# Weight splits for the next large products, queued ahead of a small expert's activation

## The chip, the cores and the metric

One core of a Trainium2 chip runs the whole program as one launch. The metric is the device time of that launch in microseconds, as the median of several runs. Five engines matter here: TensorE (PE, with its weight loads as PEld), VectorE (DVE), ScalarE (ACT), GpSimd (POOL) and SyncE (SP), whose queue issues nearly all weight loads.

## The reference, cut to what matters

A two-layer encoder trunk on 512 tokens of width 1024. Each layer ends with a mixture of 16 experts; a router gives every token two of them. Only the experts are touched here:

```python
y = zeros((512, 1024))
for e in range(16):
    he = silu(t @ w_gate[e]) * (t @ w_up[e])          # 1024 -> 512
    y = y + combine[:, e:e + 1] * (he @ w_down[e])    # 512 -> 1024
```

All data are fp32. The weights of one expert are 6 MB, so a layer's experts read about 100 MB.

## The kernel before, in words

**Experts in an order of their own.** The tokens of an expert are gathered by index (an indirect DMA issued by GpSimd), multiplied, and added to the output by an indirect scatter. The experts run at positions 0 to 15. Their order is drawn up so that experts with few tokens ("few": at most 64 rows, or at most 32) stand between those with more ("full": a 128-row tile). The program holds one branch for each of several mixes of sizes. With these inputs layer 0 takes the branch 15: few experts at positions 0, 6, 12 and 13 (64 rows) and 3, 5, 8, 10, 14 and 15 (32 rows). Layer 1 takes the branch 12: few experts (64 rows) at positions 0, 1, 2, 5, 8, 11, 14 and 15.

**Two products for each expert.** `A` is the first one (gate and up), `B` the second one (down). `A(e + 1)` is put into the program before `B(e)`, so that the activation of one expert lies beside a product of another. Inside `A(e + 1)` a call `mid` turns (transposes) the activated rows of expert `e`; inside `B(e)` it turns the gathered rows of `e + 2`.

**Full experts** (`stageA`, `stageB`) multiply in a fast fp32 format, in which one product is made of three: each weight slab of 128x1024 is split into a rounded part `wh` (a copy on ScalarE, L110) and a rest `wl` (a subtraction on VectorE, L111). `A` needs eight splits (four steps of gate and up), `B` four. Step `k` of a product can't start before its split. The parts live in two small pools (`wsp`, three tiles each of `wh` and `wl`; `wsp2`, two each), from which `spool()` deals in turn, so that five splits can be alive at a time. The matmuls are at L1018 to L1023 (`A`) and L1049 (`B`).

**Few experts** (`Few.a`, `Few.b`) use the raw weights, side by side in column groups of TensorE (L1092), and need no split. After the first product ScalarE applies silu (L1106) and VectorE multiplies by the up part and the token's weight (L1107); TensorE then turns the result `he` (L1079).

**Who sets the order on an engine.** The framework's planner puts all instructions of a branch into one queue for each engine, by their place in the program and by its own estimate of when each is ready. An engine then runs its queue in that order. `self.after(x, y)` is an edge that only says: `x` goes behind `y` in the queue. It adds no semaphore.

**Loads.** Each expert's 12 slabs of 512 KB are issued by SP (L122) in a fixed order, each into the slot of an earlier slab, so a load waits until that slab's last reader is done: for a full expert the split, for a few expert the matmul.

Of the kernel before, what the change touches and what calls it, by code (L numbers as in the profile page):

```python
# [8 lines left out]
F32 = mybir.dt.float32  # L9
# [3 lines left out]
AF = mybir.ActivationFunctionType  # L13
ALU = mybir.AluOpType
# [7 lines left out]
NE = 16  # L22
# [22 lines left out]
MB = 1  # L45
# [15 lines left out]
SM = (32, 64)  # L61
# [6 lines left out]
class Net:  # L68
# [37 lines left out]
    def split(self, raw, pool=None, tags=("wh", "wl")):  # L106

        nc = self.nc
        h, l = ((pool or self.wsp).tile([128, 1024], F32R, tag=t, name=self.nm("w" + c)) for t, c in zip(tags, "hl"))
        nc.scalar.copy(h, raw)  # L110
        nc.vector.tensor_tensor(l, raw, h.bitcast(F32), ALU.subtract)  # L111
        return h, l

    def wload(self, src, pool=None, tag="w", t=None):
# [792 lines left out]
    def moe(self, l, base, dst, g2):  # L907
        nc, tc, a, m = self.nc, self.tc, self.a, self.mo
# [7 lines left out]
        def spool():  # L916
            si[0] += 1
            return self.wsp2 if si[0] % (HB + HD) >= HB else self.wsp
# [75 lines left out]
        def bank(tag="mm"):  # L994
            return self.mm.tile([128, 512], F32, tag="mm", name=self.nm("mo"))

        def stageA(c, XT, G, U, mid=None, more=None, he=None):
            XT, full = XT
            pg, pu = bank(), bank()
            t = None  # L1000
            for kp in range(4):
                if kp == MA and mid:
                    t = mid()
                if 2 * kp not in full:
                    gh, gl = self.split(G[kp], spool())
                    uh, ul = self.split(U[kp], spool())
                if more and kp == 0:
                    more.turn()
                for kk in range(2):
                    k = kp * 2 + kk  # L1010
                    s = slice(kk * 512, (kk + 1) * 512)
                    st, sp = (k == 0), (k == NK - 1)
                    if k in full:
                        nc.tensor.matmul(pg, full[k], G[kp][:, s], start=st, stop=sp)
                        nc.tensor.matmul(pu, full[k], U[kp][:, s], start=st, stop=sp)
                        continue
                    xh, xl = XT[k // 4][:, 0, k % 4, :], XT[k // 4][:, 1, k % 4, :]
                    nc.tensor.matmul(pg, xh, gh[:, s], start=st, stop=False)  # L1018
                    nc.tensor.matmul(pg, xh, gl[:, s], start=False, stop=False)  # L1019
                    nc.tensor.matmul(pu, xh, uh[:, s], start=st, stop=False)  # L1020
                    nc.tensor.matmul(pu, xh, ul[:, s], start=False, stop=False)
                    nc.tensor.matmul(pg, xl, gh[:, s], start=False, stop=sp)  # L1022
                    nc.tensor.matmul(pu, xl, uh[:, s], start=False, stop=sp)  # L1023
                    if more:
                        more.a(k, (gh[:, s], gl[:, s]), (uh[:, s], ul[:, s]))
            he = act(c, pg, pu, he)
            if more:
                more.act()
            return he, t
# [1 line left out]
        def heT(he, mode=BA, f=2):  # L1031
            return turn(he, 4, "heT", fix[f:f + 1], mode[1])

        def stageB(c, ht, Dn, mid=None, at=MB, more=None, yo=None):
            (t,), full = ht
            pd = [bank(), bank()]
            r, parts = None, []
            for f in range(4):
                if f == at and mid:
                    r = mid()  # L1040
                st, sp = f == 0, f == 3
                if f in full:
                    tri = ((full[f], Dn[f]),)
                else:
                    dh, dl = self.split(Dn[f], spool())
                    tri = ((t[:, 0, f], dh), (t[:, 0, f], dl), (t[:, 1, f], dh))
                for i, (x, y) in enumerate(tri):
                    for h in range(2):
                        nc.tensor.matmul(pd[h], x, y[:, h * 512:(h + 1) * 512], start=(st and i == 0),  # L1049
                                         stop=(sp and i == len(tri) - 1))  # L1050
                if more:
                    parts.append((f, dh, dl))
            finish(c, pd, yo)
            if more:
                more.b(parts)
                more.end()
            return r
# [6 lines left out]
        class Few:  # L1064
# [27 lines left out]
                    nc.tensor.matmul(ps[r, 0:w], x, ys[i // k][:, (i % k) * w:(i % k + 1) * w], start=st, stop=sp,  # L1092
                                     tile_position=(0, r.start))

            def a(u, G, U, mid=None):
                ps, t = bank(), None
                for kp in range(4):
                    if kp == MA and mid:
                        t = mid()
                    for kk in range(2):  # L1100
                        k, s = kp * 2 + kk, slice(kk * 512, (kk + 1) * 512)
                        u.beside(ps, u.xt[:, k], (U[kp][:, s], G[kp][:, s]), k == 0, k == NK - 1)
                w, h = 8 * u.n, len(u.at) // 2
                for i in range(h):
                    s = slice(i * w, (i + 1) * w)
                    nc.scalar.activation(u.he[:, s], ps[u.at[h + i], 0:w], AF.Silu)  # L1106
                    nc.vector.scalar_tensor_tensor(u.he[:, s], ps[u.at[i], 0:w], u.w[u.o], u.he[:, s], ALU.mult, ALU.mult)  # L1107
                return t

            def b(u, Dn, mid=None):  # L1110
# [63 lines left out]
        he = m.tile([128, 512], F32, tag="he", name=self.nm("he"), bufs=1)  # L1174
# [10 lines left out]
        def rest(v):  # L1185

            ti, lv, more = [0], v % 10 // 2, v % 2
# [7 lines left out]
            if more:  # L1195
                sp = [t.rearrange("p (a k n) -> p a k n", a=2, k=4) for t in own]
            Ws, Ds, Xs = {0: W[0], 1: W[1]}, {0: D0}, {0: X0, 1: X1}
            units = {}

            def nxt(n):  # L1200
                ti[0] += n
# [10 lines left out]
            def job(p):  # L1212
                if p not in jobs:
                    y = self.yt if p < NE - 1 else self.xg[(p - 1) % XG]
                    jobs[p] = Few(few[p], seq[p], self.xg[p % XG], 0, he, y, last=int(p == NE - 1), yo=64 * (p % 2))
                return jobs[p]

            def turnX(p):
                if p >= NE:
                    return None  # L1220
                if p in few:
                    job(p).turn()
                    return None
                return xT(Xs[p])

            def turnH(p):
                if p in few:
                    job(p).turn2()
                    return None
                r = heT(he, BA, 2 if p < NE - 1 else 1)  # L1230
                if p in units:
                    units[p].turn2()
                return r

            def A(p, XT, mid):
                un = units.get(p)
                if p in few:
                    return job(p).a(*Ws[p], mid)
                full = un if isinstance(un, Full) else None
                _, t = stageA(seq[p], XT, *Ws[p], mid, full, he)  # L1240
                if un and not full:
                    un.turn()
                    un.a(*Ws[p])
                return t

            def B(p, ht, mid):
                if p in few:
                    return job(p).b(Ds[p], mid)
                un = units.get(p)
                full = un if isinstance(un, Full) else None  # L1250
                y = self.xg[(p - 1) % XG] if p == NE - 1 else None
                r = stageB(seq[p], ht, Ds[p], mid, MB, full, y)
                if un and not full:
                    un.b(Ds[p])
                return r
# [3 lines left out]
            XT = turnX(1)  # L1259
# [4 lines left out]
            for e in range(NE):  # L1264
                if e:
                    next(steps, None)
                if e + 1 < NE:
                    h = A(e + 1, XT, lambda: turnH(e))
                    Ds[e + 1] = load(*which(e + 1), nxt(4), 1)[2]
                if e + 3 < NE:  # L1270
                    loadW(e + 3)
                if e == 0:
                    nc.sync.dma_start(self.g2, g2.partition_broadcast(128))
                if e < NE - 2:
                    Xs[e + 2] = get(e + 2, seq[e + 2], few.get(e + 2, 128))
                if e == 5 and more:
                    for i in (1, 0):
                        nc.gpsimd.memset(xtra[i], 0.0)
                        gather(NE + i, xtra[i])
                    units[at[NE - 1]] = Full(NE, xtra[0], sp)  # L1280
                    units[at[NE - 2]] = Few(64, NE + 1, xtra[1], 0)
                    units[at[NE - 3]] = Few(32, NE + 1, xtra[1], 64, idx=self.ovt[3])
                if e < NE - 2:
                    XT = B(e, h, lambda: turnX(e + 2))
                elif e == NE - 2:
                    h = B(e, h, lambda: turnH(e + 1))
                else:
                    B(e, h, None)

# [223 lines left out]
```

## Time and profile before

| | |
|---|---|
| runs (3) | median 1272.02 us, 1269.14 to 1276.51 |
| profiled execution | 1273.83 us, span 1272.1 us, mean granted clock 0.937 |
| PE busy | 1129.4 us (89%), 5992 matmuls |
| DVE busy | 771.0 us (61%) |
| ACT busy | 528.1 us (42%) |
| moved by DMA | 336.79 MB |

The profiled execution's own time is its span and 1.7 us around it. The experts' stages lie at about 366 to 632 us (layer 0) and 982 to 1256 us (layer 1). In a row of a timeline stand start, duration, engine, line, operation, out<-in, shape and count; in brackets, the idle time of the engine before it and what ended it.

### The profile page before, as it was taken

How to read it: one execution, taken by the hardware profiler on the slowest of the kernel's cores; microseconds unless marked ns; L12 is line 12 of the kernel's file. 1: busy time of each engine (PE TensorE's matmuls, PEld its weight loads, DVE VectorE, ACT ScalarE, POOL GpSimd, SP SyncE). 2: the span in 40 equal slices, each digit the busy share in tenths (PEclk: the TensorE clock that was granted, in tenths of full speed). 3: DMA queues.
4: the chain of work that ended last, by engine and by line, in shares of the span. 5: the costliest groups of instructions: out<-in, count | busy, mean ns of one | idle time of the engine just before them, and what ended most of it. 6: DMA issues, size and time to landing. Idle time of an engine off the chain costs nothing. (4 is left out here: it accounts for less than half of the span.)

```text
span 1272.1 us, 17590 instructions
## 1 busy us (share of the span) xinstructions
PE 1129.4 (89%) x5992; PEld 764.2 (60%) x5992; DVE 771.0 (61%) x1309; ACT 528.1 (42%) x893; POOL 157.4 (12%) x243
## 2 busy tenths in 40 slices
PE   5999979989859989999759999999993999989894
PEld 3786548878627745565357666766672366656561
DVE  3687679364669754553353789566466376666751
ACT  3325633323236533332144565466441255555530
POOL 2000000010322221111200000000123112211101
PEclk9999969999769989999979999999896999999997
DMA  9986457854569999998883564514468899999981
GB/s 347 360 310 201 145 179 239 292 189 147 170 187 409 360 361 397 386 384 313 293 319 107 167 205 152 197 50 150 157 222 244 330 400 373 383 362 385 356 333 30
DMA packets 96576, 336.79 MB, mean 265 GB/s; under 512 B 13828, under 2 KB 13892, under 8 KB 96340
## 3 DMA queue, kind: packets, MB, share of 16 engines
q1 hardware_dynamic: 85764, 308.59, 65.3%
q0 software_dynamic: 10416, 25.33, 8.5%
q10 hardware_dynamic: 288, 1.57, 0.3%
q8 instruction: 51, 0.84, 0.3%
q14 instruction: 57, 0.47, 0.1%
HBM read 319.13 MB, written 24.81 MB: 270 GB/s over the span
## 5 line engine op out<-in xcount | busy, mean ns | idle before, releaser
L110 ACT CAST wh<-w 128x1024 fp32r<-128x1024 f32 x168 | 172.4, 1050 | 198.2 <-PE mm L281 130.8
L111 DVE TENSOR_TENSOR wl<-w,wh 128x1024 fp32r<-128x1024 f32 x168 | 200.8, 1222 | 78.1 <-ACT wh L110 73.8
L281 PE MATMUL mm<-wh,hT 128*128 128x512 f32 x448 | 143.8, 396 | 1.4 <-DVE Q L578 0.8
L1092 PE MATMUL mo<-w,fewT 128*32 128x256 f32 (+1 forms) x884 | 130.1, 489 | 2.1 <-ACT fewT L1080 1.3
L281 PE MATMUL mm<-hT,wh 128*128 128x512 f32 x384 | 125.7, 402 | 0.0
L169 DVE SCALAR_TENSOR_TENSOR w<-w,cs,w 128x1024 f32<-128x1024 f32 x70 | 89.8, 1282 | 26.2 <-DMA w<-ada_w 25.3
L281 PEld LDWEIGHTS mm<-wh,hT 128*128 128x128 f32 x448 | 84.3, 189 | 21.3 <-issue 2.4
L281 PE MATMUL mm<-wl,hT 128*128 128x512 f32 x224 | 88.8, 396 | 0.0
L281 PEld LDWEIGHTS mm<-hT,wh 128*128 128x128 f32 x384 | 71.7, 190 | 17.5 <-issue 2.9
L1092 PEld LDWEIGHTS mo<-w,fewT 128*32 128x32 f32 (+1 forms) x884 | 41.7, 124 | 65.4 <-issue 48.6
L111 DVE TENSOR_TENSOR wl<-we,wh 128x1024 fp32r<-128x1024 f32 x62 | 73.6, 1222 | 9.5 <-ACT wh L110 8.7
L281 PE MATMUL mm<-hT,wl 128*128 128x512 f32 x192 | 76.8, 401 | 0.0
L110 ACT CAST wh<-we 128x1024 fp32r<-128x1024 f32 x62 | 62.4, 1048 | 20.2 <-PE mo L1022 14.1
L1049 PE MATMUL mo<-wh,fix 128*128 128x512 f32 x224 | 67.3, 408 | 2.4 <-ACT wh L110 2.4
L1092 PE MATMUL mo<-we,fewT 128*64 128x512 f32 (+1 forms) x388 | 68.0, 515 | 0.0
L636 DVE TENSOR_TENSOR_SCAN O<-O,sep 128x1284 f32<-128x1284 f32 x16 | 44.4, 2819 | 22.6 <-ACT O L632 22.6
L945 POOL DMA_INDIRECT x<-hbuf,gidxp x26 | 30.4, 1169 | 193.4 <-PE tr L1079 103.6
L1018 PE MATMUL mo<-wh,fix 128*128 128x512 f32 x112 | 47.1, 420 | 5.0 <-ACT wh L110 5.0
L1019 PE MATMUL mo<-wl,fix 128*128 128x512 f32 x112 | 45.9, 410 | 6.1 <-DVE wl L111 6.1
L1049 PEld LDWEIGHTS mo<-wh,fix 128*128 128x128 f32 x224 | 41.8, 192 | 14.5 <-ACT wh L110 3.3
L281 PEld LDWEIGHTS mm<-wl,hT 128*128 128x128 f32 x224 | 42.3, 189 | 8.7 <-issue 1.0
L969 ACT CAST fix<-tr 128x512 fp32r<-128x512 f32 x42 | 23.8, 588 | 56.5 <-PE tr L960 34.6
(361 smaller groups left out, 2049.6 us busy)
## 6 DMA issues: line engine op xcount, KB each, us to landing
w<-ada_w SPq DMA_DIRECT2D x96, 512.0 KB
w<-w_up SPq DMA_DIRECT2D x80, 512.0 KB
w<-w_down SPq DMA_DIRECT2D x80, 512.0 KB
w<-w_gate SPq DMA_DIRECT2D x79, 512.0 KB
we<-w_gate SPq DMA_DIRECT2D x46, 512.0 KB
we<-w_up SPq DMA_DIRECT2D x44, 512.0 KB
we<-w_down SPq DMA_DIRECT2D x43, 512.0 KB
w<-even_w_in SPq DMA_DIRECT2D x28, 512.0 KB
```

The costliest lines, as they stand in the source:

```text
L110: nc.scalar.copy(h, raw)
L111: nc.vector.tensor_tensor(l, raw, h.bitcast(F32), ALU.subtract)
L169: nc.vector.scalar_tensor_tensor(acc, w, self.cs[:, k:k + 1], acc, ALU.mult, ALU.add)
L281: nc.tensor.matmul(ps[m], x, y, start=(first and i == 0), stop=(last and i == 2))
L636: dve.append(nc.vector.tensor_tensor_scan(O[:, ::-1], O[:, ::-1], self.sep[:, ::-1], 0.0, ALU.mult, ALU.add))
L945: nc.gpsimd.indirect_dma_start(out=X[0:n], out_offset=None, in_=self.hbuf[0:S, :], in_offset=bass.IndirectOffsetOnAxis(ap=col(c)[0][0:n], ...
L969: nc.scalar.copy(H[:, 0, a:b], pt[:, a:b])
L1018: nc.tensor.matmul(pg, xh, gh[:, s], start=st, stop=False)
L1019: nc.tensor.matmul(pg, xh, gl[:, s], start=False, stop=False)
L1049: nc.tensor.matmul(pd[h], x, y[:, h * 512:(h + 1) * 512], start=(st and i == 0), stop=(sp and i == len(tri) - 1))
L1092: nc.tensor.matmul(ps[r, 0:w], x, ys[i // k][:, (i % k) * w:(i % k + 1) * w], start=st, stop=sp, tile_position=(0, r.start))
```

## The change

At the head of each step `e`, before `A(e + 1)`, the program now asks whether `e + 1` is a few expert. If it is, some weight splits that used to follow are put in front of it:

- If `e` is full, the first splits of its `B(e)`: all four when `e + 1` has 64 rows, two when it has 32. `stageB` takes them ready-made (`parted`).
- If `e` is a few expert too and `e + 2` is full, the first splits of `A(e + 2)`: four (two steps) or two (one step). They wait in `partA`.

Two edges for each activation piece put silu on ScalarE behind the last of these copies, and the multiplication on VectorE behind the last of these subtractions (`behind`). `split` stores its two instructions in `last_split` for that. No instruction, transfer or tile is added or removed.

```diff
@@ split
-        nc.scalar.copy(h, raw)
-        nc.vector.tensor_tensor(l, raw, h.bitcast(F32), ALU.subtract)
+        self.last_split = nc.scalar.copy(h, raw), nc.vector.tensor_tensor(l, raw, h.bitcast(F32), ALU.subtract)
@@ stageA
-                    gh, gl = self.split(G[kp], spool())
-                    uh, ul = self.split(U[kp], spool())
+                    gh, gl, uh, ul = parted[kp] if kp < len(parted) else [t for w in (G[kp], U[kp]) for t in self.split(w, spool())]
@@ stageB
-                    dh, dl = self.split(Dn[f], spool())
+                    dh, dl = parted[f] if f < len(parted) else self.split(Dn[f], spool())
@@ Few.a
-                    nc.scalar.activation(u.he[:, s], ps[u.at[h + i], 0:w], AF.Silu)
-                    nc.vector.scalar_tensor_tensor(u.he[:, s], ps[u.at[i], 0:w], u.w[u.o], u.he[:, s], ALU.mult, ALU.mult)
+                    for x, y in zip((nc.scalar.activation(u.he[:, s], ps[u.at[h + i], 0:w], AF.Silu),
+                                     nc.vector.scalar_tensor_tensor(u.he[:, s], ps[u.at[i], 0:w], u.w[u.o], u.he[:, s],
+                                                                    ALU.mult, ALU.mult)), behind or ()):
+                        self.after(x, y)
@@ rest, at the head of step e
+                parted, behind = (), None
                 if e + 1 < NE:
-                    h = A(e + 1, XT, lambda: turnH(e))
+                    if e + 1 in few:
+                        n = 4 if few[e + 1] == SM[1] else 2
+                        if e not in few:
+                            parted = [self.split(d, spool()) for d in Ds[e][:n]]
+                            behind = self.last_split
+                        elif e + 2 < NE and e + 2 not in few:
+                            partA[e + 2] = [[t for w in (Ws[e + 2][0][k], Ws[e + 2][1][k]) for t in self.split(w, spool())]
+                                            for k in range(n // 2)]
+                            behind = self.last_split
+                    h = A(e + 1, XT, lambda: turnH(e), behind)
...
-                    XT = B(e, h, lambda: turnX(e + 2))
+                    XT = B(e, h, lambda: turnX(e + 2), parted)
```

## Rows read from the trace of the kernel before

**Rows 1.** The page's costliest groups: splits and the large products (count, busy, mean, idle).

```profile
L110 ACT CAST wh<-w 128x1024 fp32r<-128x1024 f32 x168 | 172.4, 1050 | 198.2 <-PE mm L281 130.8
L111 DVE TENSOR_TENSOR wl<-w,wh 128x1024 fp32r<-128x1024 f32 x168 | 200.8, 1222 | 78.1 <-ACT wh L110 73.8
...
L1049 PE MATMUL mo<-wh,fix 128*128 128x512 f32 x224 | 67.3, 408 | 2.4 <-ACT wh L110 2.4
...
L1018 PE MATMUL mo<-wh,fix 128*128 128x512 f32 x112 | 47.1, 420 | 5.0 <-ACT wh L110 5.0
L1019 PE MATMUL mo<-wl,fix 128*128 128x512 f32 x112 | 45.9, 410 | 6.1 <-DVE wl L111 6.1
```

**Rows 2.** Timeline of PE in layer 1 around position 8.

```profile
1104.85 1.94 PE L1092 MATMUL mo<-w,fewT 128*64 128x512 f32 x8
...
1110.19 3.65 PE L1092 MATMUL mo<-w,fewT 128*64 128x512 f32 x16
1115.32 0.33 PE L1079 MATMUL tr<-ident,he 64*128 64x64 f32 x2 [1.47 <-DVE he L1107]
...
1124.98 0.50 PE L1019 MATMUL mo<-wl,fix 128*128 128x512 f32 x1 [1.82 <-DVE wl L111]
```

**Rows 3.** Timeline of ACT in the same stretch.

```profile
1113.89 0.59 ACT L1106 ACTIVATE he<-mo 64x512 f32<-64x512 f32 x1 [3.01 <-PE mo L1092]
1114.39 1.98 ACT L110 CAST wh<-w 128x1024 fp32r<-128x1024 f32 x2
```

**Rows 4.** Timeline of DVE in the same stretch.

```profile
1119.11 1.22 DVE L111 TENSOR_TENSOR wl<-we,wh 128x1024 fp32r<-128x1024 f32 x1
1122.51 1.29 DVE L991 TENSOR_TENSOR x<-mo,x 128x512 f32<-128x512 f32 x2 [2.17 <-PE mo L1049]
```

**Rows 5.** Timeline of PE in layer 1 at position 14.

```profile
1232.05 0.33 PE L1079 MATMUL tr<-ident,he 64*128 64x64 f32 x2 [1.47 <-DVE he L1107]
...
1233.47 0.73 PE L1049 MATMUL mo<-wl,fix 128*128 128x512 f32 x2 [0.17 <-DVE wl L111]
```

**Rows 6.** Timeline of PE in layer 0: positions 6 to 8, 10, and the stage's end.

```profile
464.72 0.46 PE L1079 MATMUL tr<-ident,we 32*128 32x32 f32 x5 [2.67 <-DMA we<-hbuf,gidxx]
...
468.64 0.80 PE L1018 MATMUL mo<-wh,fix 128*128 128x512 f32 x1 [1.76 <-ACT wh L110]
470.30 0.80 PE L1019 MATMUL mo<-wl,fix 128*128 128x512 f32 x1 [0.87 <-DVE wl L111]
...
498.49 0.30 PE L1079 MATMUL tr<-ident,he 32*128 32x32 f32 x2 [1.03 <-DVE he L1107]
...
542.16 0.74 PE L1049 MATMUL mo<-wh,fix 128*128 128x512 f32 x2 [2.37 <-ACT wh L110]
...
630.52 0.64 PE L1092 MATMUL mo<-w,fewT 128*32 128x256 f32 x8 [0.81 <-DMA w<-w_down]
```

**Rows 7.** Timeline of ACT in layer 0 at position 5.

```profile
442.30 2.00 ACT L110 CAST wh<-w 128x1024 fp32r<-128x1024 f32 x2
444.62 0.38 ACT L1106 ACTIVATE he<-mo 32x256 f32<-32x256 f32 x1 [0.33 <-PE mo L1092]
```

**Rows 8.** Windows: stretch, busy (x) of PE, PEld, DVE, ACT, POOL; clock; DMA share; GB/s.

```profile
570.00:580.00 10.00, 10.00 (x75) 6.50 (x73) 2.54 (x5) 1.78 (x3) 0.98 (x1) 1.00 0.59 231
580.00:590.00 10.00, 10.00 (x54) 4.94 (x51) 6.50 (x9) 5.98 (x8) 1.97 (x2) 1.00 1.01 350
1230.00:1240.00 10.00, 8.36 (x31) 5.89 (x28) 5.55 (x5) 5.23 (x7) 0.00 (x0) 0.83 0.52 187
```

**Rows 9.** Waits of SP's queue from 560 to 577 us (total, times, longest).

```profile
SPq L122 <- PE tr L1079: 8.3, 1, 8.3
```

**Rows 10.** Timeline of PE in layer 1: the last product.

```profile
1253.61 1.89 PE L1092 MATMUL mo<-we,fewT 128*64 128x512 f32 x8
```

**Rows 11.** Timeline of PE in layer 1 at the start of position 10's first product.

```profile
1144.05 0.49 PE L1018 MATMUL mo<-wh,fix 128*128 128x512 f32 x1 [1.62 <-ACT wh L110]
1145.36 0.65 PE L1019 MATMUL mo<-wl,fix 128*128 128x512 f32 x1 [0.81 <-DVE wl L111]
```

More of the change, by code (lines that the diff above doesn't have):

```diff
@@ L995, in bank, with stageA @@
             return self.mm.tile([128, 512], F32, tag="mm", name=self.nm("mo"))
-        def stageA(c, XT, G, U, mid=None, more=None, he=None):
+        def stageA(c, XT, G, U, mid=None, more=None, he=None, parted=()):
             XT, full = XT
@@ L1032, in heT, with stageB @@
             return turn(he, 4, "heT", fix[f:f + 1], mode[1])
-        def stageB(c, ht, Dn, mid=None, at=MB, more=None, yo=None):
+        def stageB(c, ht, Dn, mid=None, at=MB, more=None, yo=None, parted=()):
             (t,), full = ht
@@ L1093, in beside, with a @@
                                      tile_position=(0, r.start))
-            def a(u, G, U, mid=None):
+            def a(u, G, U, mid=None, behind=None):
                 ps, t = bank(), None
@@ L1197, in rest @@
             Ws, Ds, Xs = {0: W[0], 1: W[1]}, {0: D0}, {0: X0, 1: X1}
-            units = {}
+            units, partA = {}, {}
             def nxt(n):
@@ L1233, in turnH, with A @@
                 return r
-            def A(p, XT, mid):
+            def A(p, XT, mid, behind=None):
                 un = units.get(p)
                 if p in few:
-                    return job(p).a(*Ws[p], mid)
+                    return job(p).a(*Ws[p], mid, behind)
                 full = un if isinstance(un, Full) else None
-                _, t = stageA(seq[p], XT, *Ws[p], mid, full, he)
+                _, t = stageA(seq[p], XT, *Ws[p], mid, full, he, partA.pop(p, ()))
                 if un and not full:
@@ L1244, in A, with B @@
                 return t
-            def B(p, ht, mid):
+            def B(p, ht, mid, parted=()):
                 if p in few:
@@ L1251, in B @@
                 y = self.xg[(p - 1) % XG] if p == NE - 1 else None
-                r = stageB(seq[p], ht, Ds[p], mid, MB, full, y)
+                r = stageB(seq[p], ht, Ds[p], mid, MB, full, y, parted)
                 if un and not full:
@@ L1283, in rest @@
                 if e < NE - 2:
-                    XT = B(e, h, lambda: turnX(e + 2))
+                    XT = B(e, h, lambda: turnX(e + 2), parted)
                 elif e == NE - 2:
-                    h = B(e, h, lambda: turnH(e + 1))
+                    h = B(e, h, lambda: turnH(e + 1), parted)
                 else:
```

## The prediction

> **What bounds the kernel now.** I read the page's groups first. All the time that TensorE idles because a large expert product lacks a split is there: 2.4 us before L1049, 5.0 before L1018, 6.1 before L1019 [rows 1]; a few tenths more at L1049. That is some 14 us, so the change can't be worth much more than that, plus what such pauses cost elsewhere. A split is 1.05 us on ScalarE and 1.22 us on VectorE [rows 1].
>
> The timelines of the three engines in layer 1 at position 8 show how a pause comes about. The small product ends at 1113.85 (1110.19 + 3.65), and TensorE then stands for 1.47 us until `he` is there, because its queue has the turns of `he` ahead of position 7's large product [rows 2]. ScalarE waited 3.01 us for that small product, did silu, and began the casts right behind it [rows 3]. So nothing held these casts but the activation ahead of them; engine and weights were free. The late splits then push everything: VectorE sits 2.17 us behind the finish of the large product (L991) with further splits queued behind it [rows 4], and position 9's first product stands 1.82 us for a `wl` [rows 2].
>
> Then the windows. In layer 0 the DMA share is 1.01 at 580 to 590 but 0.59 at 570 to 580 [rows 8], where SP waited 8.3 us for TensorE to let go of a slot [rows 9]. At the stage's end TensorE waits for the last `w_down` [rows 6]. So layer 0 ends by its transfers, and TensorE's time is worth there only what it gives back to the DMA. In layer 1 the share has fallen to 0.52 by 1230 to 1240, while the last slab is used from 1253.61 on [rows 8, 10]: transfers end some 14 us ahead of their use, and layer 1 ends by TensorE.
>
> **The change part by part.** It adds and removes no instruction and no DMA. It moves 36 splits: in layer 0 two each at positions 3, 5, 8 and 10, four at 12, and four of position 7's first product at 6; in layer 1 four each at 5, 8, 11 and 14, and four of position 3's at 2. The silu pieces go behind them.
>
> *Where no pause stood,* the worth is nothing: in layer 0 positions 3, 5 and 12, in layer 1 positions 2 and 5. At position 5 two casts stand ahead of silu already [rows 7]; the order asked for is partly the old one. The cover there is the small product, and if it were gone, two splits would cost 2 x 1.22 = 2.4 us a place.
>
> *Layer 1, positions 8 and 11.* The four casts take about 4 x 1.0 us (two took 1.98 [rows 3]), the four subtractions 4.9 us. The small product takes 9.0 us (1104.85 to 1113.85 [rows 2]), so they fit beside it. Position 7's product can then start at 1113.85, and the turns of `he` go behind it; VectorE is about four splits ahead, so position 9's first step isn't late either. Worth 1.47 + 1.82 = 3.29 us. The same pair of pauses stands at position 11: twice 3.29 = 6.6 us. The two bounds are 1.47 each (the second pause stays) and 3.29 each; I take the latter, because that pause was made by splits that are now done.
>
> *Layer 1, position 14.* Pauses of 1.47 and 0.17 us [rows 5]. The granted clock is 0.83 at 1230 to 1240, the window in which the pauses lie [rows 8]; that is a mean of its two levels, 1.2 and 2.4 GHz. At 0.83 of full speed 10 us lose 1.7 us of work. If the pause goes, I expect the clock to stay. Together 3.3 us; lower bound 1.6, if the clock falls anyway.
>
> Layer 1: 6.6 + 3.3 = 9.9 us, below the 14 us by which its transfers are ahead.
>
> *Layer 0.* TensorE gets back 1.76 + 0.87 at position 7, 1.03 at 8 and 2.37 at 10, in all 6.0 us [rows 6]. But the stage ends by the DMA, whose only large hole that TensorE makes is the one at 570 to 580: (1.01 - 0.59) x 10 = 4.2 us. With TensorE 6.0 us ahead by then, SP's wait of 8.3 us is over before the transfers run dry. Raw slabs also come free earlier, since a slab of a full expert is free after its split. So layer 0 is worth 4.2 us and no more: bounds 0 (another holder of that slot is late) and 4.2.
>
> *The added wait.* Silu now stands on ScalarE behind splits, which wait for weights and for free split tiles. Queued behind it are the copies of the turned `he` and the next splits; TensorE's turns of `he` wait for it, and behind them the small second product and its scatter. The tightest place is position 6 in layer 0, where position 7's weights have just been loaded. The trace of before doesn't show when a slab landed, so: at least 0, at most a full row of four subtractions, 4.9 us. TensorE waits 2.67 us there for a gather anyway [rows 6], so 2.2 us at most come out, and layer 0's end by the DMA covers these. I take 0.
>
> The Trainium skill (TensorE: Matmul & The Clock Gate, section "Architectural detail: the array is 16× 32×32, not 1× 128×128") calls ScalarE and VectorE strict FIFO. This is the rule that speaks against this change: whatever holds a split now holds silu too, and by it the sum could turn into the last rival below. That silu and the finish at L991 kept splits waiting behind them agrees with it [rows 3, 4].
>
> **The sum.** 9.9 + 4.2 = 14.1 us off the profiled execution's 1273.83 us gives 1259.7. That execution is 1.8 us above the median of the runs; from 1272.02 it is 1257.9. I predict 1259 us.
>
> **The rivals,** each counted from the median of 1272.0 us.
>
> *Layer 1 alone.* The hole in layer 0's transfers stays, because the slot hangs on something that isn't earlier. For it: only one wait of SP is named [rows 9], and the planner may order that stretch anew. Against it: the name is TensorE's, and TensorE is early. 1272.0 - 9.9 = 1262 us.
>
> *Layer 0 alone.* In layer 1 the planner keeps the turns of `he` ahead of the large product, so the activation's chain (silu, product, turn) still stands there. For it: that was its order before [rows 2]. Against it: it orders by readiness, and the splits are now ready first. 1272.0 - 4.2 = 1268 us, within what can't be told from no change.
>
> *No change.* The pauses go but the planner's new order opens others; one of 1.62 + 0.81 us stands at a place that the change doesn't touch [rows 11]. About 1272 us.
>
> *More than the sum.* The new order takes such pauses along: two of them in layer 1, each 2.4 us and a stretch at 0.83 of the clock (1.7 us): 8.2 us more, 1251 us.
>
> *Slower: the splits hold the activation.* If the splits start only when the small product ends (no free split tile, or no weights), the product behind silu waits for four of them: 1.0 + 4 x 1.22 = 5.9 us, a pause that long instead of 1.47 wherever the turns stay ahead. At positions 8, 11 and 14 that is 3 x 4.4 = 13.3 us more: 1285 us. It begins to cost once the splits start more than 9.0 - 4.9 = 4.1 us into the small product. Against it: the casts ran the moment silu let them [rows 3], and TensorE had finished the previous large product before the small one began.
>
> **How the numbers follow.** About 0.5% (6.4 us) is what a measurement of this kernel can tell from no change; faster means below 1265.7, slower above 1278.4. Chances: the forecast 0.52, layer 1 alone 0.12, more than the sum 0.05: faster 0.69. Layer 0 alone 0.10 and no change 0.13: same 0.23. Slower 0.08. The range goes from 1251 (more than the sum) to 1269 (layer 0 alone, and 1 us for the scatter of the runs); no change and slower, 0.21, are left out.
>
> **What would show it.** On ScalarE and VectorE four splits stand ahead of silu at positions 8, 11 and 14 of layer 1, within the small product. On TensorE L1049 follows L1092 without a pause, the turns of `he` come after, the pauses before L1019 behind positions 8 and 11 are gone, and the clock is 1.00 behind position 14. In layer 0 the DMA share at about 565 to 575 is 1.0, SP's wait of 8.3 us is much shorter, and the last TensorE instruction still waits for `w_down`, 4 us earlier. Idle time by group falls to about 5 us from 14. The prediction is wrong if silu starts late behind splits that wait, if the turns of `he` still stand ahead of L1049, or if TensorE gains its pauses in layer 0 and the stage doesn't end earlier.

## The result, and the profile after

The changed kernel takes **1257.8 us** (median of 4 runs, 1257.2 to 1263.2), the kernel before on the same chip 1271.6 us: a ratio of 0.9896, 95% interval 0.9856 to 0.9936. Two later sets of runs of the same pair gave 0.9894 [0.9861, 0.9927] and 0.9907 [0.9877, 0.9938]. So it is faster by about 13 us, and the prediction of 1259 us (1251 to 1269) holds the time. But the profiled executions differ by 10.7 us (1273.83 and 1263.16): the three traced executions of the changed kernel lie 3 to 5 us above the medians of their runs, that of before 2 us above. And the sum behind the prediction isn't the sum that the traces show: one of its terms failed, and another came by a way that wasn't foreseen.

The line numbers moved: both halves of a split are at L110 now, the large products at L1016 to L1021 (`A`) and L1047 (`B`), the small ones at L1090, their turn and its copy at L1077 and L1078, silu and the multiplication at L1104 and L1105.

The page's costliest groups of after (they answer [rows 1]):

```profile
L110 ACT CAST wh<-w 128x1024 fp32r<-128x1024 f32 x168 | 172.4, 1049 | 201.0 <-PE mm L280 128.2
L110 DVE TENSOR_TENSOR wl<-w,wh 128x1024 fp32r<-128x1024 f32 x168 | 201.0, 1222 | 81.0 <-ACT wh L110 77.0
L1090 PE MATMUL mo<-w,fewT 128*32 128x256 f32 (+1 forms) x884 | 130.3, 492 | 4.7 <-DMA w<-w_down 3.2
L1047 PE MATMUL mo<-wh,fix 128*128 128x512 f32 x224 | 65.8, 400 | 1.7 <-ACT wh L110 1.7
L1017 PE MATMUL mo<-wl,fix 128*128 128x512 f32 x112 | 46.8, 418 | 5.7 <-DVE wl L110 5.7
L1016 PE MATMUL mo<-wh,fix 128*128 128x512 f32 x112 | 47.2, 421 | 3.2 <-ACT wh L110 3.2
```

Counts stand, and busy times nearly so. The idle time for splits has fallen by 0.7 us (L1047), 1.8 (L1016) and 0.4 (L1017) only: what fell most, the waits of the turns for `he` (8.8 us before, 2.6 after), isn't in these groups, and L1090 now waits 3.2 us for `w_down`.

**Layer 1, position 8.** Timelines of after, TensorE, then ScalarE and VectorE (they answer [rows 2 to 4]):

```profile
1105.97 3.65 PE L1090 MATMUL mo<-w,fewT 128*64 128x512 f32 x16
1109.56 0.73 PE L1047 MATMUL mo<-wh,fix 128*128 128x512 f32 x2
...
1115.49 0.46 PE L1077 MATMUL tr<-ident,he 64*128 64x64 f32 x4
...
1117.60 0.50 PE L1017 MATMUL mo<-wl,fix 128*128 128x512 f32 x1 [0.40 <-DVE wl L110]
```

```profile
1106.56 2.94 ACT L110 CAST wh<-w 128x1024 fp32r<-128x1024 f32 x3
1109.40 1.05 ACT L110 CAST wh<-we 128x1024 fp32r<-128x1024 f32 x1
1110.47 0.60 ACT L1104 ACTIVATE he<-mo 64x512 f32<-64x512 f32 x1
```

```profile
1107.64 3.50 DVE L110 TENSOR_TENSOR wl<-w,wh 128x1024 fp32r<-128x1024 f32 x3 [0.25 <-ACT wh L110]
...
1115.13 1.29 DVE L990 TENSOR_TENSOR x<-mo,x 128x512 f32<-128x512 f32 x2 [2.20 <-PE mo L1047]
```

The reader sees what the prediction described: four casts beside the small product and ahead of silu, the large product right behind the small one, the turns of `he` behind that. Of 1.47 + 1.82 us, 0.40 is left. VectorE still stands 2.20 us behind the finish with splits queued behind it, but it is ahead by then. Position 11 shows the same.

**Layer 1, position 14.** ScalarE and TensorE of after (answering [rows 5]):

```profile
1221.43 0.59 ACT L1078 COPY fewT<-tr 128x512 f32<-128x512 f32 x1 [7.33 <-PE mo L1090]
1221.92 1.99 ACT L110 CAST wh<-t 128x1024 fp32r<-128x1024 f32 x2
1223.81 2.00 ACT L110 CAST wh<-w 128x1024 fp32r<-128x1024 f32 x2
1225.84 0.59 ACT L1104 ACTIVATE he<-mo 64x512 f32<-64x512 f32 x1
```

```profile
1214.27 7.09 PE L1090 MATMUL mo<-we,fewT 128*64 128x512 f32 x32
1223.02 0.72 PE L1047 MATMUL mo<-wh,fix 128*128 128x512 f32 x2 [1.65 <-ACT wh L110]
1224.28 0.74 PE L1047 MATMUL mo<-wl,fix 128*128 128x512 f32 x2 [0.54 <-DVE wl L110]
```

Here the pause stayed. ScalarE's queue has one more thing ahead of the four casts: the copy of position 15's turned rows. It writes the tile that the small product reads, so it waits 7.33 us for that product, and the casts wait behind it.

**Layer 0, the end.** Timelines of TensorE, VectorE and GpSimd, of after, then of before:

```profile
611.00 0.24 PE L1077 MATMUL tr<-ident,he 32*128 32x32 f32 x1 [1.00 <-DVE he L1105]
...
624.33 0.64 PE L1090 MATMUL mo<-w,fewT 128*32 128x256 f32 x8 [1.80 <-DMA w<-w_down]
626.38 3.42 PE L1090 MATMUL mo<-w,fewT 128*32 128x256 f32 x24 [1.41 <-DMA w<-w_down]
644.60 5.42 PE L249 MATMUL tr<-dg,x 128*128 128x128 f32 x24 [14.81 <-DVE dg L236]
...
629.89 1.76 DVE L1119 TENSOR_TENSOR x<-mo,x 32x256 f32<-32x256 f32 x4 [5.50 <-PE mo L1090]
...
625.14 1.35 POOL L983 DMA_INDIRECT xbuf<-x,gidxp  x1 [6.71 <-DVE x L1119]
631.92 1.32 POOL L983 DMA_INDIRECT xbuf<-x,gidxp  x1 [5.43 <-POOLq L1331]
```

```profile
616.86 0.24 PE L1079 MATMUL tr<-ident,he 32*128 32x32 f32 x1 [1.25 <-DVE he L1107]
...
648.69 3.54 PE L250 MATMUL tr<-dg,x 128*128 128x128 f32 x15 [17.54 <-DVE dg L237]
...
631.25 1.76 DVE L1119 TENSOR_TENSOR x<-mo,x 32x256 f32<-32x256 f32 x4 [0.98 <-PE mo L1092]
...
631.03 1.34 POOL L984 DMA_INDIRECT xbuf<-x,gidxp  x1 [6.73 <-DVE x L1119]
635.25 1.65 POOL L984 DMA_INDIRECT xbuf<-x,gidxp  x1 [2.88 <-POOLq L1321]
```

TensorE's work on layer 0's experts begins at 366.43 before and at 367.96 after. So position 14's turns come 250.4 us into the stage before and 243.0 us after: 7.4 us are won. At the stage's end (631.15 and 629.79, 264.7 and 261.8 us in) 2.9 us of them are left; the rest went into the waits for `w_down`. But layer 1 begins sooner behind it: 14.81 us in place of 17.54. Before, the last finish is done at 633.01 and its scatter starts at 635.25, behind a scatter that began at 631.03; after, the last scatter follows its finish (629.89 + 1.76) by 0.27 us, because the scatter ahead of it began 6.8 us before it, and not 4.2 us as in the kernel before.

Windows of after (columns as in [rows 8]):

```profile
570.00:580.00 10.00, 10.00 (x79) 4.27 (x79) 6.34 (x11) 5.09 (x7) 2.33 (x2) 1.00 1.01 373
...
1130.00:1140.00 10.00, 7.61 (x32) 3.62 (x29) 6.54 (x8) 5.55 (x8) 2.48 (x2) 0.89 0.98 373
...
1190.00:1200.00 10.00, 7.62 (x23) 5.69 (x22) 8.89 (x9) 7.40 (x8) 1.42 (x1) 0.66 1.01 384
...
1230.00:1240.00 10.00, 9.38 (x47) 3.25 (x48) 1.48 (x3) 1.34 (x3) 1.57 (x1) 1.00 0.49 130
```

The window of before that holds position 13's start:

```profile
1200.00:1210.00 10.00, 7.62 (x30) 5.59 (x27) 9.34 (x10) 7.75 (x9) 1.46 (x1) 0.83 1.03 392
```

The hole in layer 0's transfers is gone (1.01 for 0.59), and SP's wait for TensorE there is 1.2 us in place of 8.3. The clock behind position 14 is 1.00, as forecast; behind position 13 it is 0.66, where before it was 0.83.

### The profile page after: what moved, and what is told of

It reads as the page before. It is cut to its first block, busy times and chain, and to the rows that moved or that the text cites. A ratio compares the mean times of both kernels' runs of the same rounds, so it can differ in the third digit from the quotient of the medians.

```text
span 1261.4 us, 17596 instructions
## 1 busy us (share of the span) xinstructions
PE 1128.2 (89%) x5992; PEld 765.8 (61%) x5992; DVE 769.1 (61%) x1309; ACT 527.5 (42%) x893; POOL 155.7 (12%) x243
## 5 line engine op out<-in xcount | busy, mean ns | idle before, releaser
L110 ACT CAST wh<-w 128x1024 fp32r<-128x1024 f32 x168 | 172.4, 1049 | 201.0 <-PE mm L280 128.2
L110 DVE TENSOR_TENSOR wl<-w,wh 128x1024 fp32r<-128x1024 f32 x168 | 201.0, 1222 | 81.0 <-ACT wh L110 77.0
L1090 PE MATMUL mo<-w,fewT 128*32 128x256 f32 (+1 forms) x884 | 130.3, 492 | 4.7 <-DMA w<-w_down 3.2
L1090 PEld LDWEIGHTS mo<-w,fewT 128*32 128x32 f32 (+1 forms) x884 | 41.8, 124 | 67.2 <-issue 49.0
L280 PEld LDWEIGHTS mm<-hT,wh 128*128 128x128 f32 x384 | 71.7, 190 | 17.5 <-issue 3.0
L110 DVE TENSOR_TENSOR wl<-we,wh 128x1024 fp32r<-128x1024 f32 x62 | 73.5, 1221 | 12.9 <-ACT wh L110 12.5
L110 ACT CAST wh<-we 128x1024 fp32r<-128x1024 f32 x62 | 62.6, 1048 | 17.5 <-PE mo L1020 15.7
L1090 PE MATMUL mo<-we,fewT 128*64 128x512 f32 (+1 forms) x388 | 67.3, 506 | 0.0
L1047 PE MATMUL mo<-wh,fix 128*128 128x512 f32 x224 | 65.8, 400 | 1.7 <-ACT wh L110 1.7
L1078 ACT COPY fewT<-tr 128x256 f32<-128x256 f32 (+2 forms) x40 | 16.9, 423 | 84.2 <-PE tr L1077 69.5
L1017 PE MATMUL mo<-wl,fix 128*128 128x512 f32 x112 | 46.8, 418 | 5.7 <-DVE wl L110 5.7
L1047 PEld LDWEIGHTS mo<-wh,fix 128*128 128x128 f32 x224 | 40.8, 188 | 15.9 <-ACT wh L110 5.4
L1016 PE MATMUL mo<-wh,fix 128*128 128x512 f32 x112 | 47.2, 421 | 3.2 <-ACT wh L110 3.2
## 6 DMA issues: line engine op xcount, KB each, us to landing
we<-w_down SPq DMA_DIRECT2D x43, 512.0 KB, 10.6
```

The source lines that it names most:

```text
L110: self.last_split = nc.scalar.copy(h, raw), nc.vector.tensor_tensor(l, raw, h.bitcast(F32), ALU.subtract)
L280: nc.tensor.matmul(ps[m], x, y, start=(first and i == 0), stop=(last and i == 2))
L1078: nc.scalar.copy(dst, pt)
```

## The experiments

Apart from ratios I read three lengths in each trace, because that is where the change acts: **stage 0** and **stage 1** (from TensorE's first turn of a gathered row to the end of its last expert product, in each layer) and the **gap** from the end of stage 0 to TensorE's next instruction. A stage of one execution scatters by some 1.5 us either way.

| kernel | stage 0 | gap | stage 1 | ratio to before |
|---|---|---|---|---|
| before | 264.7 | 17.5 | 273.0 | 1 |
| changed (three executions) | 261.8, 263.8, 263.2 | 14.8, 15.4, 15.0 | 266.3, 265.4, 265.6 | 0.9896, 0.9894, 0.9907 |
| layer 1 only | 265.1 | 17.4 | 265.3 | 0.9920 [0.9891, 0.9948] |
| layer 0 only | 261.7 | 14.7 | 271.7 | 0.9963 [0.9938, 0.9988] |
| without the edges | 262.0 | 17.8 | 271.0 | 1.0023 [0.9996, 1.0049] |
| copy behind, ready-made second products | 262.3 | 14.7 | 262.6 | 0.9874 [0.9840, 0.9909] |
| copy behind, everywhere | 261.0 | 15.4 | 261.0 | 0.9891 [0.9857, 0.9925] |
| ahead of the finish too | 261.8 | 14.6 | 260.6 | 0.9852 [0.9819, 0.9885] |
| two splits | 261.1 | 14.8 | 262.4 | one execution |

**The changed kernel again, and its two halves.** The edit of the halves, with 0 for 1 in the other:

```diff
-                    if e + 1 in few:
+                    if l == 1 and e + 1 in few:
```

> The changed kernel once more, nothing edited, as the measure for the others. Its profiled execution was 1263.2 us and its other runs 1257.2 to 1257.9. If the two late waits for w_down at the end of layer 0 (1.80 and 1.41 us) belong to that one execution, the new profile has less than 1.5 us there and a time of 1257 to 1259; if they belong to the kernel, they stand again and the time is again above 1260 under the profiler. Ratio to the kernel before 0.986 to 0.993.

> The change in layer 1 alone. By the prediction's sum 9.9 us off (ratio 0.9922). By the trace of the changed kernel, where position 14 kept a pause of 2.2 us, 6.6 us off (ratio 0.9948). Rival, that layer 0 carries nothing and layer 1 all: the whole gain, 13 to 14 us (0.989).

> The change in layer 0 alone. By the prediction's sum 4.2 us off (ratio 0.9967), because the end of that stage is set by the transfers. By what TensorE gets back there without such a bound, 6.0 us off (0.9953). Rival, that its end doesn't move: less than 1 us (0.999 to 1.001).

The waits for `w_down` belong to the kernel: they stand in all its executions. Layer 1 alone gives 0.9920, layer 0 alone 0.9963, about 10 and 5 us: both halves carry, and the rivals that gave all to one fall. The interval of layer 1 alone holds both values that were expected for it (0.9922 and 0.9948), so the time doesn't decide between them; the lengths do. From these: with the change in layer 1 stage 1 is 265.3 to 266.3 us, without it 271.0 to 273.0, so 6.2 us between the means. With the change in layer 0 the gap is 14.6 to 15.4, without it 17.4 to 17.8: 2.6 us. Stage 0 falls from a mean of 263.9 (three executions without) to 262.1 (eight with): 1.8 us, less sure because 262.0 also came without. Together 10.6 us. The profiled pair's own three lengths differ by 12.3 us; in the changed kernel layer 0's stage began 1.5 us later, and so the whole differs by 10.7.

**The loads at layer 0's end.**

```diff
-                    Ds[e + 1] = load(*which(e + 1), nxt(4), 1)[2]
+                    Ds[e + 1] = Ds[e] if l == 0 and e >= 13 else load(*which(e + 1), nxt(4), 1)[2]
```

> The kernel before, with the eight w_down loads of layer 0's last two positions left out (their second products use position 13's slabs). If the kernel before ends layer 0 by TensorE and transfers nearly together, TensorE's stage (first turn to last product of layer 0) is 264 us, at most 1 us below its 264.7. If the transfers alone set its end, it is 4 us or more below.

> The changed kernel, with the same eight loads left out. In the traces so far TensorE reaches the last turns of he in layer 0 7.4 us earlier than before, counted from the stage's start, and ends only 2.9 us earlier. If the transfers of w_down take the rest (the prediction's cap), the stage falls to 257 to 258 us, 6 to 7 us below the same kernel before with the loads left out. Rival, that the gain is given back by TensorE's own order at the stage's end: 261 to 262 us, as with the loads.

Without these loads (the last two second products use position 13's slabs) stage 0 is 264.3 us in the kernel before and 256.2 us in the changed one, one execution each: 8.1 us apart, where with the loads it is 1.8. So TensorE does win some 8 us in layer 0, and the transfers of `w_down` take most of it back. The prediction's cap stood for the changed kernel; its rival, TensorE's own order at the end, falls. But in the kernel before the stage is 0.4 us shorter without the loads (264.7 to 264.3). So its layer 0 didn't end by transfers alone, as the prediction had it: TensorE and the transfers ended nearly together, and the transfers became the limit when TensorE got faster.

The same execution of the kernel before also bears on the gap. Its last two scatters:

```profile
628.73 1.34 POOL L984 DMA_INDIRECT xbuf<-x,gidxp  x1 [3.99 <-DMA xbuf<-x,gidxp]
634.61 1.33 POOL L984 DMA_INDIRECT xbuf<-x,gidxp  x1 [4.54 <-POOLq L1321]
```

They start 5.9 us apart, the last one 0.27 us behind its finish, and the gap is 15.2 us, as in the changed kernel. So the gap shrinks without the change too, once the last scatter but one starts early enough.

**The edges.**

```diff
-                        self.after(x, y)
+                        pass
```

> The changed kernel without the edges that put silu and the multiplication behind the splits; the splits stay ahead of the small product in the program. If the planner goes by place in the program, ScalarE has four splits ahead of silu at positions 8 and 11 of layer 1 all the same, and the time is that of the changed kernel within 1.5 us. Rival, that it goes by its own estimate of readiness and the edges do the work: silu goes ahead of the splits again, the pauses of 1.47 and 1.82 us are back at both positions, and the time is 6 us or more above the changed kernel.

The rival holds. ScalarE and TensorE of this kernel at position 8:

```profile
1113.90 0.59 ACT L1104 ACTIVATE he<-mo 64x512 f32<-64x512 f32 x1 [3.01 <-PE mo L1090]
1114.39 1.98 ACT L110 CAST wh<-w 128x1024 fp32r<-128x1024 f32 x2
...
1115.32 0.33 PE L1077 MATMUL tr<-ident,he 64*128 64x64 f32 x2 [1.47 <-DVE he L1105]
1124.97 0.51 PE L1017 MATMUL mo<-wl,fix 128*128 128x512 f32 x1 [1.82 <-DVE wl L110]
```

These are [rows 2, 3] over again, at the same times and with the same pauses, though the splits stand ahead in the program. A place in the program buys nothing here; the planner puts silu first unless an edge forbids it. Without the edges nothing of the gain is left. Edges with the splits at their old place weren't tried.

**The copy at position 14.** In `Few.turned`, with `lead` the last ready-made cast, or none:

```diff
-                nc.scalar.copy(dst, pt)
+                c = nc.scalar.copy(dst, pt); self.lead and self.after(c, self.lead)
```

> The changed kernel, and ScalarE's copy of the turned rows of the next expert (which waits for the small product) goes behind the splits that are ready-made for the second product; this bears on position 14 of layer 1 and position 12 of layer 0. If that copy is what held the four casts at position 14, they lie within the small product, the pauses of 1.65 and 0.54 us go, and the time is 2 to 2.5 us below that of the changed kernel run beside it. Rival, that the casts wait for their weights or for free split tiles: the casts start no earlier than 1221 us and the time is the same within 0.5 us.

```profile
1211.60 1.99 ACT L110 CAST wh<-t 128x1024 fp32r<-128x1024 f32 x2
1213.49 1.99 ACT L110 CAST wh<-w 128x1024 fp32r<-128x1024 f32 x2
1219.00 0.59 ACT L1104 ACTIVATE he<-mo 64x512 f32<-64x512 f32 x1 [3.52 <-PE mo L1090]
1219.62 0.59 ACT L1078 COPY fewT<-tr 128x512 f32<-128x512 f32 x1
```

That copy was the cause: the casts lie within the small product, no pause is left at position 14, and the time is 1255.9 us against 1259.0 for the changed kernel beside it, 3.1 us less (2 to 2.5 expected). The intervals of the two ratios overlap; what shows the cause is the trace. Stage 1 is 3.2 us below the mean of the changed kernel's.

**The same copy at positions 10 and 13**, with `lead` also the first step's last cast where a full expert follows (of these places only positions 10 and 13 had pauses in layer 1):

> As the kernel with the copy behind the splits at position 14, and the same at the starts of positions 10 and 13 of layer 1, where the copy of the next small expert's turned rows stands ahead of the first two splits on ScalarE. The casts can then begin at 1133.9 in place of 1135.57, behind the last cast of he; the pause of 1.62 us goes at both places. But VectorE finishes the small product (1134.71 to 1136.12) ahead of the first subtraction, so the wait for wl grows from 0.77 to about 1.8: 0.6 us gained a place, 1 us together and up to 2 with the clock. Rival, that the whole pair of pauses goes: 4.8 us and the clock, 6 us or more.

As expected: one pause of 1.95 us for `wl` at either place, in place of 1.62 and 0.77, and stage 1 1.6 us shorter. The times of this kernel and the last come from different sets of runs, the intervals of their ratios overlap, and they can't be told apart.

**Ahead of the finish too.** The first two splits of positions 10 and 13 are put ahead of the small second product before them (the edit does the same wherever two full experts follow a small one); the cast of the turned `he` (ScalarE) and the finish of that product (VectorE) go behind them by edges. The first line is for the cast, the second for the finish:

```diff
+                c = nc.scalar.copy(H[:, 0, a:b], pt[:, a:b]); tag == 'heT' and self.hold and self.after(c, self.hold[0])
...
+                    d = nc.vector.tensor_tensor(u.y[:, s], pd[r, 0:w], self.g2[r, s], ALU.mult); self.hold and self.after(d, self.hold[1])
```

> As the kernel with the copy behind the splits at every place, and at positions 10 and 13 of layer 1 the first two splits go ahead of two more things: on ScalarE the cast of the turned he, on VectorE the finish of the small product before. The casts can begin at about 1130 and the subtractions end by about 1133.5, before TensorE is through with the small product (1135). If these two were what held them, both pauses of 1.95 us go: TensorE's stage of layer 1 falls from 261.0 us by 3.9 us and up to 2 us of clock, to 255 to 257 us, and the time by as much. Rival one, that the weights or the free split tiles are late there: the stage stays at 260 to 261.5. Rival two, that layer 1 now ends by its transfers: the pauses go but waits for w_gate, w_up or w_down appear behind position 13.

> The changed kernel a third time, as the measure for the kernel beside it: TensorE's stage of layer 1 265 to 266.5 us, of layer 0 261.5 to 264 us, ratio to the kernel before 0.986 to 0.993.

TensorE's last waits in this kernel, and three windows (columns as in [rows 8]):

```profile
1223.07 1.94 PE L1090 MATMUL mo<-w,fewT 128*64 128x512 f32 x8 [0.59 <-DMA w<-w_up]
1226.70 1.94 PE L1090 MATMUL mo<-w,fewT 128*64 128x512 f32 x8 [1.69 <-DMA w<-w_up]
...
1232.45 2.30 PE L1090 MATMUL mo<-w,fewT 128*64 128x512 f32 x8 [0.66 <-DMA w<-w_down]
```

```profile
1130.00:1140.00 10.00, 10.00 (x48) 5.94 (x45) 8.62 (x10) 7.44 (x9) 2.48 (x2) 1.00 0.98 375
...
1190.00:1200.00 10.00, 10.00 (x46) 8.04 (x45) 8.56 (x9) 6.67 (x8) 0.00 (x0) 1.00 1.03 389
...
1220.00:1230.00 10.00, 7.04 (x32) 1.68 (x28) 0.69 (x1) 0.59 (x1) 1.29 (x1) 1.00 1.01 358
```

Both pauses are gone and the clock is 1.00 in every window from 1110 to 1240. Yet stage 1 fell by 0.4 us, not by 3.9 to 6: TensorE now waits for `w_up` and `w_down` behind position 13, with the DMA share at 1.01. That is the second rival: layer 1 has come to end by its transfers. The share alone wouldn't show it: in the kernel before it is 0.96 to 1.04 in every window from 1000 to 1230, and TensorE doesn't wait for weights there. At 1254.8 us, against 1260.0 for the changed kernel beside it, this version is ahead of both kernels, and its six runs all lie below those of the changed kernel. Its ratio is the lowest of the table, but the intervals of the two versions with the copy behind overlap with it.

**First products, and the number of splits.** The one leaves out the splits made ahead for first products (and the loads, as above), the other has `n = 2` throughout:

> The changed kernel without the splits that are made ahead for a first product (positions 6 and 7 of layer 0, 2 and 3 of layer 1), and without the eight w_down loads at the end of layer 0, so that TensorE's time shows there. With the splits for first products that stage took 256.2 us and TensorE waited 3.1 us for a wl at position 7, with silu of position 6 some 8 us late behind splits that waited for weights. If that late silu costs nothing and the earlier splits help, the pauses of the kernel before come back (2.6 for the gather, 1.5 and 0.9 for splits, 5.0 in all) and the stage is 258 us. Rival, that silu behind waiting splits costs more than it brings: 255 us or less.

> The changed kernel with two splits ahead of every small expert's activation in place of four for one of 64 rows. Two splits cover the first 2.8 us of the second product (12 matmuls), and the third and fourth follow silu, which is off TensorE's path by then. If all that counts is that the first splits don't wait behind silu, layer 1's stage is 265 to 266.5 us as with four. Rival, that the number counts because the splits of the next first product come later: the pauses of 1.82 us at positions 9 and 12 are back and the stage is 268 to 269.5 us.

Without the splits for first products stage 0 is 262.1 us, not 258, one execution: 5.9 us above the kernel with them, not 2. The pauses of 2.4, 1.5 and 0.9 us are back in place of one of 3.1, as expected; what was left out is the clock, 0.62 at 465 to 475 us against 1.00. From 460 to 480 us the clock costs 5.1 us here and 1.7 there. As two executions of the changed kernel lose 3.4 and 1.7 us in the same stretch with the same order, only the 2 us of pauses are sure to be the splits' worth. With two splits in place of four stage 1 is 262.4 us, below the 265 to 266.5 expected: the 0.40 us behind positions 8 and 11 are gone too. So the number beyond two brings nothing. That two are better by 3 us isn't shown: 1.7 us of it is the clock behind position 13 (0.92 and 0.91 in two windows, 1.7 us lost, where 0.66 loses 3.4), which also differed between kernels of the same order up to there, and the changed kernel waits 0.95 to 1.45 us for gathered rows at the stage's start, this one not at all. What is left is the 0.8 us of the two pauses.

## Why the prediction was right, point by point

**Positions 8 and 11** were forecast at 6.6 us and gave 2.9 each, 5.8: mechanism, place and order as written, 0.40 us left at each. The bound of 3.29 was the better of the two. But the working had set its ceiling by the three groups of the large products, 13.5 us, and expected 5 us to be left there. They still hold 10.6 us; the pauses of 1.47 us stood in the group of the turns, which it hadn't counted in.

**Position 14 is the step that failed** ("If the pause goes, I expect the clock to stay. Together 3.3 us"). The pauses grew from 1.64 to 2.19 us. The working had only silu ahead of the casts and missed the copy of the next small expert's turned rows. The lower bound of 1.6 was too high as well, as it assumed that the pause goes. The Trainium skill's rule that ScalarE and VectorE are strict FIFO (TensorE: Matmul & The Clock Gate, section "Architectural detail: the array is 16× 32×32, not 1× 128×128") agrees with this row: one copy that waited 7.33 us held four casts whose engine was free. The clock did stay at 1.00 there, but it dipped deeper behind position 13 (0.66), so that from 1110 to 1250 the windows lose 5.1 us to it before and after alike: of the 1.7 us nothing came. Layer 1 in all: 6.2 us for 9.9. (5.8 less 0.55 is 5.2; the other 1 us stands in no pause of the rows, and what it is stays open.)

**Layer 0** was forecast at 4.2 us, by the hole in the transfers, and gave 1.8 in its stage and 2.6 in the gap, 4.4. That the transfers cap it was right, and the runs without loads show it. The size wasn't: the hole of 4.2 us was filled, and less than half of it reached the stage's end. That the total still comes to 4.4 is luck. The gap wasn't foreseen: TensorE's lead lets the last scatter but one start earlier, and the last one no longer queues behind it. The kernel before without its last loads agrees (5.9 us between the two, gap 15.2); no run moved that scatter alone.

**The added wait.** TensorE and ScalarE of after at positions 6 and 7 of layer 0:

```profile
466.04 0.79 PE L1017 MATMUL mo<-wl,fix 128*128 128x512 f32 x1 [3.34 <-DVE wl L110]
...
467.17 1.04 ACT L110 CAST wh<-w 128x1024 fp32r<-128x1024 f32 x1 [1.47 <-DMA w<-w_up]
468.24 0.59 ACT L1104 ACTIVATE he<-mo 64x512 f32<-64x512 f32 x1
```

Silu of position 6 came 8 us late (468.24, before 460.17) behind casts that waited 2.20, 1.26 and 1.47 us for their weights. The prediction had named a silu that starts late behind waiting splits as a sign of being wrong; here it came. I took its cost at 0, and none is to be seen: the same splits saved about 2 us of pauses. But position 7's 1.76 + 0.87 us weren't won back as forecast: together with the 2.67 us for the gather they became one wait of 3.34 us for a `wl` whose weights came late.

**The rivals.** *Slower* took place at position 14 (splits begun at 1221.92, when the small product had ended), though by the copy and not for want of tiles or weights, and at 2.2 us and not 5.9: the turns of `he` weren't ahead of the large product any more, and TensorE only had to await the first split. *Layer 0 alone* was argued against with "it orders by readiness, and the splits are now ready first"; the kernel without edges shows that this argument is wrong, and that only the edges kept that rival away. *More than the sum* wanted the pauses at position 10 and 13 to go; the kernel that removes them shows that layer 1's transfers allow little of the 8.2 us.

**The sum.** 14.1 us forecast, 10.6 by the traces, some 13 by the medians (13.8, 14.2 and 10.7), whose intervals reach 4 to 5 us either way. That the time came out within 2 us of the forecast is partly luck: position 14's 3.3 us didn't come, the gap's 2.6 us wasn't in the working, and the medians gave more than the traces.

## What to carry to other kernels

When work is moved ahead in an in-order queue, list everything that lands in front of it, not only the instruction that it was meant to pass: here a copy held the casts at one place of three. Moving it in the program may change nothing where a planner orders by its own estimates; an edge does. And before pricing the next pause, look what else ends the stage: layer 1 had some 12 us in it (273.0 to 260.6), and then the transfers set its end.

## What the runs showed of the hardware that wasn't expected

The granted clock doesn't follow the length of a pause in any simple way. Before, pauses of 1.47 and 0.17 us at position 14 went with 0.83; in the changed kernel 1.65 and 0.54 us at the same place went with 1.00. At position 13 the same pauses (1.62 and 0.76) went with 0.66 in one kernel and 0.83 (1.62 and 0.77) in the one with the copy behind at position 14, whose order up to there is the same; at position 10 it was the other way round (0.89 and 0.94 in two windows, against 0.74 and 0.92), so that both kernels lose 5.1 us to it. In the kernel ahead of the finish it stayed at 1.00 from 1110 to 1240: up to 1220 no pause there was longer than 0.52 us, and behind that one of 1.69 us left it at 1.00 too.
